# An encoder trunk: squares added on VectorE, rope and bias marks set later, modulation loaded with the latent heads

## The chip, the cores and the metric

The kernel runs on one core of one Trainium2 chip. The metric is device time in microseconds (us) of one execution. A core has several engines with queues of their own: TensorE (PE) multiplies matrices, VectorE (DVE) and ScalarE (ACT) work elementwise, SyncE (SP) issues the transfers, GpSimd (POOL) does almost nothing here. Each engine works its queue in order and waits on semaphores for the others.

## The reference

Two layers of a bidirectional encoder, for 256 tokens of width D = 2048 in float32. Each layer modulates with six vectors of 2048 values that come from one conditioning vector:

```python
cond = silu(c)
for l in range(2):
    mod = cond @ w_ada[l] + b_ada[l]            # w_ada[l]: 2048 x 12288
    sh_a, sc_a, g_a, sh_m, sc_m, g_m = split(mod, 6)
    h = rmsnorm(x) * (1 + sc_a) + sh_a
    proj = h @ w_in[l]                          # dq, dk, dv, cq, ckv, kr
    out_a = diff_attention(dq, dk, dv, positions, bias_table, lam, ...)  # 4 heads, relative bias
    q  = rmsnorm(cq, q_norm_g)  @ w_uq[l]       # latent attention: 8 heads, rope on 64 of 192
    kv = rmsnorm(ckv, kv_norm_g) @ w_ukv[l]
    out_b = mla_attention(q, rope(q), kv, rope(kr), ...)
    x = x + g_a * (concat(out_a, out_b) @ w_o[l])
    h = rmsnorm(x) * (1 + sc_m) + sh_m
    x = x + g_m * (square(relu(h @ w_mlp_in[l])) @ w_mlp_out[l])
return rmsnorm(x, final_norm_g)
```

## The kernel before

Activations lie transposed, features on the 128 partitions and the 256 tokens along the row, so that a weight tile is the fixed side of a matmul. Accuracy comes from splitting: `weights()` loads a raw float32 tile of 1 MB (2048 columns; w_f2 and w_n have 1536), ScalarE writes `hi` (L145), VectorE the remainder `lo` (L146), and `mac` (L181 to L183) does three matmuls for each 128x128 tile. Raw tiles have five buffers.

The modulation is no matmul. Each of the 192 tiles of w_ada, 1 MB, is loaded by `ada_load` (L289) into the same five buffers as the raw weights, multiplied with cond and summed along the row by one VectorE instruction in `ada_sums` (L297), followed by a short one that reads the accumulator and one that adds b_ada (L312, L314) into `mod`. `weights()` sums what has been loaded before, then adds `self.rate` to a credit and issues one such load for each whole unit of it. The rates differ by stage: RATE_H behind the head, RATE_A0 in layer 0's attention, RATE_A1 and RATE_A2 in layer 1's, RATE_K and RATE_M later. All loads go through SP's queue in the order of issue.

The order of the program in layer 0:

- `setup`, `bias_setup` (tables for the relative bias), the squares of x (ScalarE, L370, eight instructions of 128x512), `rstd` (32 matmul records with a matrix of 1/D, L580; square root; reciprocal, L583), `rope_setup` (cosine and sine, L533 to L552).
- The head: eight tiles k. Each loads two w_ada tiles of 1 MB, 0.384 MB of w_f1 and 0.512 MB of w_v1, sums the two, forms `ht` (VectorE, L381) and `hf` (ScalarE, L409), and runs 12 matmuls `pk` (L412) and 8 `pv` (L416). Behind tiles 2 and 4 stand the marks of the relative bias (`bias_marks`, 0 and 1: VectorE writes `oh`), behind 4 and 7 their products (`bias_products`, matmuls `pb`, L521 and L522, copied out as `bias` by ScalarE, L524).
- Sixteen w_b tiles of 1 MB, 48 `mac` records each.
- Layer 0: copies, `latent` for ckv, bias parts 2 and 3 (`bias_part` is marks and products together), `lambdas`, `rest_feats` (four w_f2 loads), `latent` for cq, then `probs(0)`, `keys` (w_kr and rope on the keys), `probs(1)`, two w_dv tiles, `probs(2)`, `up_k`, `probs(3)` and so on.
- The latent heads: `heads[hm]` has three steps for each of eight heads (scores, turn, values); the list `mla` puts them in ten groups so that heads overlap. The softmax there reads scores `psm` into `sm` (VectorE, L1093).
- w_oa (four tiles), w_ob (twelve tiles in pairs, residual x updated at L955 and its squares added), the norm (L580, L583, `ht` at L654) with sixteen w_n tiles, the MLP.

In setup, head and the w_b tiles, TensorE's order is the written one; on the other engines and elsewhere a scheduler orders instructions as they become ready by its own costs, inside what dependencies and buffers allow.

Of the kernel before, what the change touches and what calls it, by code (L numbers as in the profile page):

```python
# [20 lines left out]
D = 2048  # L21
# [78 lines left out]

RATE_H, RATE_A0, RATE_A1, RATE_A2, RATE_K, RATE_M = 1.25, 1.4, 0.5, 0.7, 0.6, 0.66


class Trunk:
# [31 lines left out]
    def weights(self, src, width=2048):  # L136
# [11 lines left out]
        self.ada_sums(ins)  # L148
        self.credit += self.rate
        while self.credit >= 1.0 and self.ada_todo:  # L150
            self.credit -= 1.0
            self.ada_load()
        return out

# [204 lines left out]
    def head(self):  # L359
# [5 lines left out]
        self.setup()  # L365
        self.bias_setup()
        sq = []
        for k in range(0, NK, 2):
            t = self.t("sqx")
            nc.scalar.activation(t, self.x[:, k : k + 2], AF.Square)  # L370
            sq += [t[:, 0], t[:, 1]]
        r = self.rstd(sq, D, True)
        self.rope_setup()
        sh, sc = self.mod[0, 0], self.mod[0, 1]
# [22 lines left out]
        for k in range(NSPLIT):  # L397
# [16 lines left out]
            for t in range(2):  # L414
                for cg in range(2):
                    mm(flat(vals[cg][t]), fs[k][:, t * P : (t + 1) * P], w[1][:, cg * 512 : cg * 512 + 512],  # L416
                       start=k == 0, stop=k == NSPLIT - 1)
            if k in MARKS:
                marks[MARKS[k]] = self.bias_marks(MARKS[k])
# [16 lines left out]

    def rest_feats(self, h):

        banks = self.open_banks(3)
        for p in range((NK - NSPLIT) // 2):  # L440
            for i, w in enumerate(self.weights(self.io["w_f2"][0, p], 1536)):
                k = NSPLIT + 2 * p + i
                for j in range(6):
                    self.mac(banks[j // 2][:, j % 2], w, j * P, P, h[k], k == NSPLIT and j % 2 == 0, k == NK - 1 and j % 2 == 1, True)
        qs = 1.0 / math.sqrt(128.0)
        for ps, t, s in zip(banks, self.part_f, (-1.0, qs, -1.0)):
            self.nc.vector.scalar_tensor_tensor(t, ps, s, t, ALU.mult, ALU.add)
        return self.part_f
# [123 lines left out]

    def rstd(self, acc, n, plain=False):

        nc = self.nc
        ps = self.bank("pn")[:, 0]
        if not plain:
            acc = acc[:2] + acc[3:]
        for i, a in enumerate(acc):
            nc.tensor.matmul(ps, self.mean[n], a, start=i == 0, stop=i == len(acc) - 1)  # L580
        r = self.cp.tile([P, T], F32, tag="rstd", name=self.name("rstd"), bufs=2)
        nc.scalar.activation(r, ps, AF.Sqrt, bias=self.eps)
        nc.vector.reciprocal(r, r)  # L583
        return r
# [115 lines left out]
    def layer(self, l, acc, st):  # L700
# [70 lines left out]
        for i in range(HM + 2):  # L771
            for s in range(3):
                if 0 <= i - s < HM:
                    mla.append(heads[i - s][s])
        gkv = self.vec[:, V_KVG + 2 * l : V_KVG + 2 * l + 2]
        gq = self.vec[:, V_QG + 4 * l : V_QG + 4 * l + 4]
        if l == 0:
# [3 lines left out]
            ckv += self.latent([ckr], gkv)  # L781
            self.bias_part(2)
            self.bias_part(3)
            self.lambdas()
            k2, q3, k3 = self.rest_feats(h)
            cq += self.latent(cqr, gq)
            kk += [k2, k3]
            q.append(q3)
            probs(0)()
            keys()  # L790
            probs(1)()
# [3 lines left out]
        else:  # L795
# [14 lines left out]
            self.rate = RATE_A2  # L810
        up_k()
        probs(3)()
# [19 lines left out]
        self.ada_need(l, 2, NK - 1)  # L832
        banks = self.open_banks(2)
        self.by_k(banks, [io["w_oa"][l, 0]], self.mo, 0, NK)
        for f in (av[0][1], av[1][1], av[2][0], av[3][0]):
# [386 lines left out]
```

## Time and profile before

| | us |
|---|---|
| median of 3 runs | 2275.76 (2272.86 to 2278.68) |
| the profiled execution | 2278.85 |
| its span | 2277.1 |
| TensorE busy | 2185.3 |
| VectorE busy | 1624.1 |
| ScalarE busy | 1157.1 |
| mean granted TensorE clock | 0.979 |

The profile is of one execution. Times in it count from the start of the span; durations are in us, or in ns where said. A group row gives line, engine, operation, output <- input and shape, then busy time and mean; an arrow in brackets gives the idle time before an instruction and what ended it. Accumulating instructions of VectorE show as two records, the second being the read of the accumulator. Matmuls in float32 show as more records than the program has instructions.

### The profile page before, as it was taken

Reading aid. Unit: us, or ns where it says so; the run is one execution under the profiler, and the core shown is the slowest. Engines: PE = TensorE matmul, PEld = TensorE weight load, DVE = VectorE, ACT = ScalarE, POOL = GpSimd, SP = SyncE. Lnnn points to the kernel's source line nnn. Section 1 sums busy time; section 2 is a strip of 40 time slices with the busy share of each in tenths; the row PEclk is TensorE's granted clock in tenths of the full one; section 3 lists DMA queues with packets and bytes.
Section 4 is the critical chain, followed back from the end, with each engine's and each line's share of the span. In section 5 each row is a group of like instructions: output and inputs, shape, how many; then the busy total and the mean of one; then the engine's idle time right before and its main releaser. Section 6 shows DMA issues by size and latency. Waiting matters only on the chain.

```text
span 2277.1 us, 31049 instructions
## 1 busy us (share of the span) xinstructions
PE 2185.3 (96%) x12346; PEld 1910.4 (84%) x12346; DVE 1624.1 (71%) x2161; ACT 1157.1 (51%) x1707; POOL 22.9 (1%) x43
## 2 busy tenths in 40 slices
PE   7996899879999999999999999999999999999997
PEld 4795778879888888888888898999888888888886
DVE  7786986897778778778899886677644544555555
ACT  3435565245446446445446656546645535544643
POOL 0000000000000000000001000000000000000000
PEclk9997999999999999999999999999999999999998
DMA  9795685879888888887876775665555555555551
GB/s 392 288 371 211 259 314 206 327 279 336 331 316 320 310 313 323 328 322 298 324 298 245 285 263 213 222 239 187 192 196 185 193 195 185 185 203 189 196 189 56
DMA packets 83812, 585.40 MB, mean 257 GB/s; under 512 B 9297, under 2 KB 9681, under 8 KB 17361
## 3 DMA queue, kind: packets, MB, share of 16 engines
q1 hardware_dynamic: 83666, 583.42, 69.0%
q8 instruction: 96, 1.57, 0.3%
q14 instruction: 50, 0.41, 0.1%
HBM read 581.28 MB, written 2.10 MB: 256 GB/s over the span
## 4 chain that ended last, share of the span: by engine, by line
PE 85%; DVE 9%; DMA 3%; ACT 2%; issue 1%; DVEq 0%; ACTq 0%
PE ps L202 20%; PE ps L205 11%; PE py L923 10%; PE py L925 10%; PE py L927 10%; DVE ada L297 3%; DVE lo L146 2%; PE pk L181 2%; PE pk L183 2%; PE pk L182 2%; PE ps L183 1%; PE ps L182 1%; PE ps L181 1%; DMA raw<-in_w_b 1%; PE pv L416 1%
## 5 line engine op out<-in xcount | busy, mean ns | idle before, releaser
L146 DVE TENSOR_TENSOR lo<-raw,hi 128x1024 fp32r<-128x1024 f32 (+1 forms) x724 | 854.8, 1195 | 507.2 <-ACT hi L145 346.4
L145 ACT ACTIVATE hi<-raw 128x1024 fp32r<-128x1024 f32 (+1 forms) x724 | 744.8, 1037 | 699.3 <-PE py L927 371.3
L202 PE MATMUL ps<-h,hi 128*128 128x512 f32 x2016 | 472.1, 391 | 0.0
L202 PEld LDWEIGHTS ps<-h,hi 128*128 128x128 f32 x2016 | 375.2, 188 | 75.7
L297 DVE SCALAR_TENSOR_TENSOR ada<-ada,cond 128x2048 f32<-128x2048 f32 x192 | 437.8, 2284 | 0.0
L923 PE MATMUL py<-hi,hid 128*128 128x512 f32 x1024 | 326.1, 389 | 0.0
L927 PE MATMUL py<-hi,hid 128*128 128x512 f32 x1024 | 325.7, 389 | 0.0
L925 PE MATMUL py<-lo,hid 128*128 128x512 f32 x1024 | 325.7, 389 | 0.0
L205 PEld LDWEIGHTS ps<-h,lo 128*128 128x128 f32 x2016 | 250.2, 192 | 4.9
L205 PE MATMUL ps<-h,lo 128*128 128x256 f32 x2016 | 251.7, 283 | 0.0
L927 PEld LDWEIGHTS py<-hi,hid 128*128 128x128 f32 x1024 | 192.2, 188 | 40.0
L925 PEld LDWEIGHTS py<-lo,hid 128*128 128x128 f32 x1024 | 192.2, 188 | 39.8
L923 PEld LDWEIGHTS py<-hi,hid 128*128 128x128 f32 x1024 | 191.7, 188 | 39.2
L181 PE MATMUL pk<-h,hi 128*128 128x256 f32 x496 | 141.7, 286 | 5.8 <-ACT h L655 5.8
L183 PE MATMUL pk<-h,lo 128*128 128x256 f32 x496 | 142.0, 286 | 1.7 <-DVE lo L146 1.5
L182 PE MATMUL pk<-h,hi 128*128 128x256 f32 x496 | 141.7, 286 | 0.0
L181 PEld LDWEIGHTS pk<-h,hi 128*128 128x128 f32 x496 | 96.3, 195 | 6.6 <-ACT h L655 6.2
L183 PEld LDWEIGHTS pk<-h,lo 128*128 128x128 f32 x496 | 96.6, 195 | 2.8 <-DVE lo L146 2.5
L961 ACT ACTIVATE sum<-ps 128x256 f32<-128x256 f32 x110 | 42.1, 383 | 111.6 <-PE ps L205 111.5
L182 PEld LDWEIGHTS pk<-h,hi 128*128 128x128 f32 x496 | 96.5, 195 | 0.2
L175 DVE TENSOR_TENSOR hid<-relu,hid 128x256 fp32r<-128x256 f32 x128 | 48.2, 421 | 47.1 <-ACT hid L174 47.1
L181 PE MATMUL ps<-moh,hi 128*128 128x256 f32 x192 | 55.9, 291 | 6.7 <-ACT hi L145 6.7
(240 smaller groups left out, 2614.6 us busy)
## 6 DMA issues: line engine op xcount, KB each, us to landing
raw<-in_w_m SPq DMA_DIRECT2D x238, 1024.0 KB, 4.8
ada<-in_w_ada SPq DMA_DIRECT2D x192, 1024.0 KB, 5.2
raw<-in_w_ob SPq DMA_DIRECT2D x24, 1024.0 KB, 5.7
raw<-in_w_b SPq DMA_DIRECT2D x16, 1024.0 KB, 6.8
raw<-in_w_q SPq DMA_DIRECT2D x16, 1024.0 KB, 5.1
raw<-in_w_dv SPq DMA_DIRECT2D x12, 1024.0 KB, 5.9
raw<-in_w_n SPq DMA_DIRECT2D x16, 768.0 KB, 5.9
raw<-in_w_oa SPq DMA_DIRECT2D x8, 1024.0 KB, 5.4
```

Of the source, the lines that this page charges most:

```text
L145: nc.scalar.activation(hi, v, AF.Copy)
L146: ins = nc.vector.tensor_tensor(lo, v, hi.bitcast(F32), ALU.subtract)
L175: self.nc.vector.tensor_tensor(lo, val[:, i], hi.bitcast(F32), ALU.subtract)
L181: mm(ps, hi, x[0], start=first, stop=False, skip_group_check=shared)
L182: mm(ps, hi, x[1], start=False, stop=False, skip_group_check=shared)
L183: mm(ps, lo, x[0], start=False, stop=last, skip_group_check=shared)
L202: mm(ps.rearrange("p a b -> p (a b)"), part(w, 0, k), both, start=k == 0, stop=False)
L205: mm(ps[:, 0], part(w, 1, k), x, start=False, stop=k == nk - 1)
L297: ins = nc.vector.scalar_tensor_tensor(w, w, 1.0, self.cond, ALU.mult, ALU.mult, accum_out=acc[:, i : i + 1])
L923: mm(o, xh[:, tok], hi[:, part[j]], start=start, stop=False)
L925: mm(o, xh[:, tok], lo[:, part[j]], start=False, stop=False)
L927: mm(o, xl[:, tok], hi[:, part[j]], start=False, stop=stop)
```

## The change

Squares of x: `sumsq`, which the later norms use, squares on ScalarE and adds on VectorE, so `rstd` gets two rows (L585 of the changed kernel, four records) in place of sixteen tiles, and its argument `plain` goes. `bias_setup` moves behind head tile 1, `rope_setup` out of the head into layer 0. The bias parts 2 and 3 are taken apart: marks first, products behind a half of `rest_feats`. `keys` stands ahead of `probs(0)`, and `up_k` of layer 0 ahead of `probs(1)`. In layer 0 each of the ten groups of latent-head steps ends with `tick()`, which sums the modulation tiles loaded before and adds RATE_S to the credit; RATE_A0 falls to 1.2, and from w_oa on layer 0 loads at RATE_O = 0.6.

```diff
@@ -98,7 +98,7 @@
 NNORM = 12
 
 
-RATE_H, RATE_A0, RATE_A1, RATE_A2, RATE_K, RATE_M = 1.25, 1.4, 0.5, 0.7, 0.6, 0.66
+RATE_H, RATE_A0, RATE_S, RATE_O, RATE_A1, RATE_A2, RATE_K, RATE_M = 1.25, 1.2, 1.3, 0.6, 0.5, 0.7, 0.6, 0.66
 
 
 class Trunk:
@@ -146,11 +146,18 @@
             ins = nc.vector.tensor_tensor(lo, v, hi.bitcast(F32), ALU.subtract)
             out.append((hi, lo))
         self.ada_sums(ins)
-        self.credit += self.rate
+        self.more(self.rate)
+        return out
+
+    def more(self, rate):
+        self.credit += rate
         while self.credit >= 1.0 and self.ada_todo:
             self.credit -= 1.0
             self.ada_load()
-        return out
+
+    def tick(self):
+        self.ada_sums()
+        self.more(RATE_S)
 
     def raw(self, src, width):
         raw = self.wp.tile([P, width], F32, tag="raw", name=self.name("raw"), bufs=5)
@@ -363,14 +370,10 @@
         flat = lambda ps: ps.rearrange("p a b -> p (a b)")
         qs = 1.0 / math.sqrt(128.0)
         self.setup()
-        self.bias_setup()
-        sq = []
+        acc = None
         for k in range(0, NK, 2):
-            t = self.t("sqx")
-            nc.scalar.activation(t, self.x[:, k : k + 2], AF.Square)
-            sq += [t[:, 0], t[:, 1]]
-        r = self.rstd(sq, D, True)
-        self.rope_setup()
+            acc = self.sumsq(acc, self.x[:, k : k + 2])
+        r = self.rstd(acc, D)
         sh, sc = self.mod[0, 0], self.mod[0, 1]
         feats = self.open_banks(3)
         vals = [[self.bank("pv") for _ in range(2)] for _ in range(2)]
@@ -415,6 +418,8 @@
                 for cg in range(2):
                     mm(flat(vals[cg][t]), fs[k][:, t * P : (t + 1) * P], w[1][:, cg * 512 : cg * 512 + 512],
                        start=k == 0, stop=k == NSPLIT - 1)
+            if k == 1:
+                self.bias_setup()
             if k in MARKS:
                 marks[MARKS[k]] = self.bias_marks(MARKS[k])
             if k in PRODUCTS:
@@ -434,14 +439,15 @@
                 ready(k + 2)
         return h, banks
 
-    def rest_feats(self, h):
-
-        banks = self.open_banks(3)
-        for p in range((NK - NSPLIT) // 2):
+    def rest_feats(self, h, ps, banks):
+
+        for p in ps:
             for i, w in enumerate(self.weights(self.io["w_f2"][0, p], 1536)):
                 k = NSPLIT + 2 * p + i
                 for j in range(6):
                     self.mac(banks[j // 2][:, j % 2], w, j * P, P, h[k], k == NSPLIT and j % 2 == 0, k == NK - 1 and j % 2 == 1, True)
+
+    def rest_sums(self, banks):
         qs = 1.0 / math.sqrt(128.0)
         for ps, t, s in zip(banks, self.part_f, (-1.0, qs, -1.0)):
             self.nc.vector.scalar_tensor_tensor(t, ps, s, t, ALU.mult, ALU.add)
@@ -570,12 +576,11 @@
         nc.vector.tensor_tensor(acc[2], acc[2], t, ALU.add)
         return acc
 
-    def rstd(self, acc, n, plain=False):
+    def rstd(self, acc, n):
 
         nc = self.nc
         ps = self.bank("pn")[:, 0]
-        if not plain:
-            acc = acc[:2] + acc[3:]
+        acc = acc[:2] + acc[3:]
         for i, a in enumerate(acc):
             nc.tensor.matmul(ps, self.mean[n], a, start=i == 0, stop=i == len(acc) - 1)
         r = self.cp.tile([P, T], F32, tag="rstd", name=self.name("rstd"), bufs=2)
@@ -772,6 +777,8 @@
             for s in range(3):
                 if 0 <= i - s < HM:
                     mla.append(heads[i - s][s])
+            if l == 0:
+                mla[-1] = lambda f=mla[-1]: (f(), self.tick())
         gkv = self.vec[:, V_KVG + 2 * l : V_KVG + 2 * l + 2]
         gq = self.vec[:, V_QG + 4 * l : V_QG + 4 * l + 4]
         if l == 0:
@@ -779,15 +786,22 @@
             kk += [self.copy(ps, "k", -1.0) for ps in banks[5:7]]
             q.append(self.copy(banks[7], "q", qs))
             ckv += self.latent([ckr], gkv)
-            self.bias_part(2)
-            self.bias_part(3)
-            self.lambdas()
-            k2, q3, k3 = self.rest_feats(h)
+            marks = self.bias_marks(2)
+            banks = self.open_banks(3)
+            self.rest_feats(h, (0, 1), banks)
+            self.bias_products(2, marks)
             cq += self.latent(cqr, gq)
+            marks = self.bias_marks(3)
+            self.rope_setup()
+            self.rest_feats(h, (2, 3), banks)
+            k2, q3, k3 = self.rest_sums(banks)
             kk += [k2, k3]
             q.append(q3)
+            self.bias_products(3, marks)
+            self.lambdas()
+            keys()
             probs(0)()
-            keys()
+            up_k()
             probs(1)()
             for kq in (2, 3):
                 val(0, kq)()
@@ -808,7 +822,7 @@
                     cq += self.latent(cqr, gq)
             keys()
             self.rate = RATE_A2
-        up_k()
+            up_k()
         probs(3)()
         up_q(0)
         turn(0)()
@@ -831,6 +845,8 @@
         g = self.mod[l, 2]
         self.ada_need(l, 2, NK - 1)
         banks = self.open_banks(2)
+        if l == 0:
+            self.rate = RATE_O
         self.by_k(banks, [io["w_oa"][l, 0]], self.mo, 0, NK)
         for f in (av[0][1], av[1][1], av[2][0], av[3][0]):
             f()
```

The instructions as the scheduler then orders them, with buffer numbers behind the names. VectorE at the start of the head, before (`ang`, `kk`, `rr`, `cc` are rope's, `rstd` the reciprocal, `ada` the modulation sums, `ht` the first tile's input):

```order
L297 SCALAR_TENSOR_TENSOR ada_232,macc_84<-ada_232,cond 128x2048
L540 SCALAR_TENSOR_TENSOR rr_201<-kk_200,rr_201 128x256
L583 RECIPROCAL rstd_196<-rstd_196 128x256
L540 SCALAR_TENSOR_TENSOR rr_201<-kk_200,rr_201 128x256
L312 SCALAR_TENSOR_TENSOR mod_83<-macc_84,vec 128x1
L540 SCALAR_TENSOR_TENSOR rr_201<-kk_200,rr_201 128x256 x4
L297 SCALAR_TENSOR_TENSOR ada_256,macc_82<-ada_256,cond 128x2048
L543 TENSOR_SCALAR rr_201<-rr_201 128x256
L314 TENSOR_TENSOR mod_81<-macc_82,vec 128x1
L547 TENSOR_SCALAR cc_216<-rr_201 128x256
L381 SCALAR_TENSOR_TENSOR ht_243<-x,mod_83,rstd_196 128x256
```

and now (`acc` are the additions of squares):

```order
L576 TENSOR_TENSOR acc_142<-acc_142,sqx_159 128x512
L576 TENSOR_TENSOR acc_142<-acc_142,sqx_162 128x512
L304 SCALAR_TENSOR_TENSOR ada_178,macc_82<-ada_178,cond 128x2048
L321 TENSOR_TENSOR mod_81<-macc_82,vec 128x1
L304 SCALAR_TENSOR_TENSOR ada_180,macc_84<-ada_180,cond 128x2048
L588 RECIPROCAL rstd_168<-rstd_168 128x256
L319 SCALAR_TENSOR_TENSOR mod_83<-macc_84,vec 128x1
L384 SCALAR_TENSOR_TENSOR ht_191<-x,mod_83,rstd_168 128x256
L481 TENSOR_SCALAR ih_229<-pos 128x264
```

Rope's rows and one modulation sum no longer stand around the reciprocal; two sums stand directly ahead of it, and the first tile's `ht` directly behind it.

ScalarE about head tiles 4 and 5, before (`sq` are from the bias marks, `bias` the copies of the products, `h` the splits for w_b):

```order
L508 ACTIVATE sq_430<-rel_398,K 128x512
L508 ACTIVATE sq_434<-rel_398,K 128x512
L524 ACTIVATE bias<-pb_438 32x512 x4
L409 ACTIVATE hf_384<-ht_471,mod_81 128x256
L409 ACTIVATE hf_496<-ht_497,mod_81 128x256
L388 ACTIVATE h_556<-hf_242 128x256
```

and now:

```order
L514 ACTIVATE sq_399<-rel_367,K 128x512
L514 ACTIVATE sq_403<-rel_367,K 128x512
L412 ACTIVATE hf_353<-ht_440,mod_81 128x256
L530 ACTIVATE bias<-pb_407 32x512 x4
L412 ACTIVATE hf_465<-ht_466,mod_81 128x256
L391 ACTIVATE h_525<-hf_190 128x256
```

The `hf` of the next tile stood behind the four copies of the bias products and now stands ahead of them.

VectorE in the latent heads, before (`sm` is the softmax's, `r` its reciprocal, `lo` a split of w_dv):

```order
L1093 TENSOR_SCALAR sm_2561,mxm_2562<-psm_2560 128x256
L146 TENSOR_TENSOR lo_2660<-raw_2657,hi_2659 128x1024
L146 TENSOR_TENSOR lo_2664<-raw_2657,hi_2663 128x1024
L1093 TENSOR_SCALAR sm_2561,mxm_2562<-psm_2560 128x256
L297 SCALAR_TENSOR_TENSOR ada_2587,macc_88<-ada_2587,cond 128x2048
L1015 RECIPROCAL r_2570<-tot_2569 128x2
L1093 TENSOR_SCALAR sm_2635,mxm_2636<-psm_2634 128x256
L314 TENSOR_TENSOR mod_87<-macc_88,vec 128x2
L297 SCALAR_TENSOR_TENSOR ada_2589,macc_90<-ada_2589,cond 128x2048
L1093 TENSOR_SCALAR sm_2635,mxm_2636<-psm_2634 128x256
L146 TENSOR_TENSOR lo_2764<-raw_2761,hi_2763 128x1024
```

and now:

```order
L1109 TENSOR_SCALAR sm_2547,mxm_2548<-psm_2546 128x256
L304 SCALAR_TENSOR_TENSOR ada_2773,macc_90<-ada_2773,cond 128x2048
L1109 TENSOR_SCALAR sm_2547,mxm_2548<-psm_2546 128x256
L304 SCALAR_TENSOR_TENSOR ada_2829,macc_90<-ada_2829,cond 128x2048
L1031 RECIPROCAL r_2556<-tot_2555 128x2
L146 TENSOR_TENSOR lo_2763<-raw_2760,hi_2762 128x1024
L1109 TENSOR_SCALAR sm_2626,mxm_2627<-psm_2625 128x256
L319 SCALAR_TENSOR_TENSOR mod_89<-macc_90,vec 128x2
L304 SCALAR_TENSOR_TENSOR ada_2859,macc_88<-ada_2859,cond 128x2048
L1109 TENSOR_SCALAR sm_2626,mxm_2627<-psm_2625 128x256
L146 TENSOR_TENSOR lo_2767<-raw_2760,hi_2766 128x1024
L1031 RECIPROCAL r_2635<-tot_2634 128x2
```

More modulation sums stand between the softmax's rows. In all there are 14 between the first `sm` and the last head's output, where 7 were.

VectorE in w_ob, before (`x` is the residual, `acc` its squares, `lo` the splits of w_ob):

```order
L146 TENSOR_TENSOR lo_3434<-raw_3427,hi_3433 128x1024
L297 SCALAR_TENSOR_TENSOR ada_3377,macc_88<-ada_3377,cond 128x2048
L146 TENSOR_TENSOR lo_3498<-raw_3495,hi_3497 128x1024
L314 TENSOR_TENSOR mod_87<-macc_88,vec 128x2
L146 TENSOR_TENSOR lo_3502<-raw_3495,hi_3501 128x1024
L297 SCALAR_TENSOR_TENSOR ada_3439,macc_90<-ada_3439,cond 128x2048
L955 SCALAR_TENSOR_TENSOR x<-ps_3363,mod_85,x 128x256 x2
L570 TENSOR_TENSOR acc_3356<-acc_3356,sqx_3491 128x512
L146 TENSOR_TENSOR lo_3561<-raw_3558,hi_3560 128x1024
L146 TENSOR_TENSOR lo_3565<-raw_3558,hi_3564 128x1024
L297 SCALAR_TENSOR_TENSOR ada_3506,macc_90<-ada_3506,cond 128x2048
L297 SCALAR_TENSOR_TENSOR ada_3508,macc_88<-ada_3508,cond 128x2048
```

and now:

```order
L576 TENSOR_TENSOR acc_3375<-acc_3375,sqx_3379 128x512
L146 TENSOR_TENSOR lo_3512<-raw_3509,hi_3511 128x1024
L146 TENSOR_TENSOR lo_3516<-raw_3509,hi_3515 128x1024
L304 SCALAR_TENSOR_TENSOR ada_3453,macc_88<-ada_3453,cond 128x2048
L146 TENSOR_TENSOR lo_3571<-raw_3568,hi_3570 128x1024
L971 SCALAR_TENSOR_TENSOR x<-ps_3382,mod_85,x 128x256 x2
L146 TENSOR_TENSOR lo_3575<-raw_3568,hi_3574 128x1024
L576 TENSOR_TENSOR acc_3375<-acc_3375,sqx_3505 128x512
L146 TENSOR_TENSOR lo_3637<-raw_3634,hi_3636 128x1024
L146 TENSOR_TENSOR lo_3641<-raw_3634,hi_3640 128x1024
L304 SCALAR_TENSOR_TENSOR ada_3578,macc_88<-ada_3578,cond 128x2048
```

Before, a sum followed each pair of splits, or two did; now one follows two pairs. Between the first w_ob residual and the last there are 7 sums, where 16 were.

On TensorE the two `pn` rows behind the w_b tiles were followed by the bias products and are now followed by w_f2's `mac` rows. In the norm behind w_ob, one modulation sum stood between the reciprocal and `ht`; now none does. On SP, 65 instead of 55 modulation loads stand ahead of the first w_oa tile, 3 instead of 6 between it and w_ob, 7 instead of 16 between w_ob and w_n, so 75 instead of 77 ahead of w_n.

## The prediction

> **What bounds the kernel now.** I read the page's busy table and chain first, then busy time by stage, then the waits and groups inside the stages that the change touches. Page, parts 1 and 4 (share of the span in brackets):
>
> ```profile
> PE 2185.3 (96%) x12346; PEld 1910.4 (84%) x12346; DVE 1624.1 (71%) x2161; ACT 1157.1 (51%) x1707; POOL 22.9 (1%) x43
> PE 85%; DVE 9%; DMA 3%; ACT 2%; issue 1%; DVEq 0%; ACTq 0%
> ```
>
> TensorE is idle for 2277.1 − 2185.3 = 92 us in all; a change that takes no multiplications away can win from that and from slow clock only. Where it is idle, by stage (each engine's busy us with its instruction count, then TensorE's granted clock, DMA share, GB/s):
>
> ```profile
> core 0: us, PE busy (x) PEld busy (x) DVE busy (x) ACT busy (x) POOL busy (x), PEclk, DMA share, GB/s
> 0.00:30.10 30.10, 16.34 (x41) 9.91 (x41) 17.54 (x37) 14.12 (x21) 1.02 (x9) 0.92 0.93 363
> 30.10:93.20 63.10, 60.22 (x192) 39.59 (x193) 49.45 (x84) 25.21 (x47) 0.00 (x0) 0.93 0.84 342
> 93.20:188.50 95.30, 93.61 (x769) 92.38 (x767) 83.42 (x99) 39.27 (x49) 0.00 (x0) 1.00 0.94 355
> 188.50:251.70 63.20, 42.52 (x250) 37.27 (x251) 46.66 (x71) 33.97 (x49) 0.53 (x1) 0.78 0.54 201
> 251.70:303.70 52.00, 44.58 (x242) 36.94 (x241) 50.68 (x108) 28.18 (x58) 0.00 (x0) 0.93 0.71 267
> 303.70:357.20 53.50, 48.00 (x242) 39.83 (x242) 37.60 (x74) 34.17 (x76) 0.00 (x0) 0.94 0.68 256
> 357.20:388.00 30.80, 30.80 (x236) 29.60 (x235) 21.31 (x29) 19.19 (x44) 0.00 (x0) 1.00 0.52 191
> 388.00:476.80 88.80, 75.85 (x582) 73.31 (x581) 75.21 (x89) 27.51 (x32) 0.00 (x0) 0.96 0.88 328
> 476.80:484.30 7.50, 1.40 (x4) 0.59 (x4) 6.68 (x9) 2.73 (x6) 0.00 (x0) 0.67 0.95 378
> ```
>
> The stages are: setup; the eight head tiles; the sixteen w_b tiles; bias, w_f2 and latents of layer 0; its keys and probabilities; its latent heads; w_oa; w_ob; the norm. Idle TensorE adds to 13.8 + 2.9 + 1.7 + 20.7 + 7.4 + 5.5 + 0 + 13.0 + 6.1 = 71 of the 92 us, and the change acts on these stages alone, the w_b tiles and the rest of the program keeping their order.
>
> **1. Setup and head (−5.5 us, between −2 and −9).** Rows of the timeline and one group:
>
> ```profile
> 10.35 3.74 ACT L370 ACTIVATE sqx<-x 128x512 f32<-128x512 f32 x7
> 11.02 9.18 PE L580 MATMUL pn<-sqx,mean 128*128 128x256 f32 x32 [1.20 <-ACT sqx L370]
> 22.43 1.74 DVE L583 RECIPROCAL rstd<-rstd 128x256 f32<-128x256 f32 x1
> 29.02 0.48 DVE L381 SCALAR_TENSOR_TENSOR ht<-x,mod,rstd 128x256 f32<-128x256 f32 x1
> 30.10 5.49 PE L412 MATMUL pk<-hf,w 128*128 128x256 f32 x12 [9.90 <-ACT hf L409]
> 189.72 1.10 PE L580 MATMUL pn<-acc,mean 128*128 128x256 f32 x4 [1.25 <-issue]
> L570 DVE TENSOR_TENSOR acc<-acc,sqx 128x512 f32<-128x512 f32 x2 | 1.4, 686 | 0.0
> L297 DVE SCALAR_TENSOR_TENSOR ada<-ada,cond 128x2048 f32<-128x2048 f32 x63 | 143.5, 2284 | 0.0
> L297 DVE DVE_READ_ACCUMULATOR ada<-ada,cond 128x1 f32 x62 | 5.2, 83 | 0.0
> L540 DVE SCALAR_TENSOR_TENSOR rr<-kk,rr 128x256 f32<-128x256 f32 x6 | 2.5, 413 | 0.1
> ```
>
> The 32 matmul records that sum the squares end at 11.02 + 9.18 = 20.2. Their place is taken by seven additions of 0.69 us, 4.8 us in all, that start behind the second square, near 10.9, and end at about 15.6 (the squares themselves end at 14.1); the four records of 1.10 us then end at 16.7, 3.5 us earlier. In the new order of VectorE two modulation sums (2.28 + 0.08 each) stand between the additions and the reciprocal, so it starts at 15.6 + 4.7 = 20.3 instead of 22.43 (the square root has its 2.2 us, as before from 20.2 to 22.43, beside them), and directly behind it, 1.74 us later, stands the first ht: at 22.0 instead of 29.02, because rope's rows and a third sum, which lay between the two, are gone. By the 1.1 us from ht to the first matmul, tile 0 begins at about 23.1 instead of 30.10: −7.
>
> Not all of it lasts. VectorE is full there, and what rope leaves (13 instructions, at the 0.41 of its row some 5 us, an estimate) bias_setup takes up again behind tile 1: eight instructions, four of them at the 0.69 us of the row of equal size, some 4 us. The next tiles' sums are then the pace, and the lead at tile 2 is 2 to 3 us. At tile 5 there is a second, separate gain:
>
> ```profile
> 20.00:40.00 20.00, 10.10 (x26) 6.79 (x26) 19.61 (x35) 5.41 (x8) 0.00 (x0) 0.74 1.02 424
> 65.53 0.48 DVE L381 SCALAR_TENSOR_TENSOR ht<-x,mod,rstd 128x256 f32<-128x256 f32 x1
> 66.87 2.39 ACT L524 ACTIVATE bias<-pb 32x512 f32<-32x512 f32 x4 [5.05 <-PE pb L522]
> 69.17 0.49 ACT L409 ACTIVATE hf<-ht,mod 128x256 f32<-128x256 f32 x1
> 69.71 4.53 PE L412 MATMUL pk<-hf,w 128*128 128x256 f32 x12 [2.88 <-ACT hf L409]
> 74.08 3.60 PE L416 MATMUL pv<-w,hf 128*128 128x512 f32 x8
> 77.51 2.75 PE L412 MATMUL pk<-hf,w 128*128 128x256 f32 x12
> ```
>
> Its ht is ready at 66.0, but hf waits on ScalarE behind four bias copies; in the new order hf stands ahead of them. That saves the 2.88 us wait and the 4.53 − 2.75 = 1.8 us of slow matmuls behind it, 4.7 together, of which the lead of 2 to 3 is partly the same time. I take −5.5. The shallow end (−2) is tile 5's wait with nothing of the start, the deep end (−9) is the whole 7 with the 1.8.
>
> On the slow matmuls, the Trainium skill's page "TensorE: Matmul & The Clock Gate", section "HAM oscillation — how this bites in real kernels", speaks against this change: if a short burst of matmuls waits longer than about 3.4 us for its data each time, each burst starts at half clock. The row above agrees, with a shorter wait: 4.53 instead of 2.75 us after 2.88. By that rule a head paced by VectorE in bursts of 6 us would run one tile more at 4.53: the sum below would be 2261 by the rule, and is 2259 without it.
>
> **2. Bias, w_f2 and latents, 188.5 to 251.7 (+1.8, between −6 and +4).** Waits of TensorE in the stage (total, times, longest):
>
> ```profile
> PE pb L521 <- DVE oh L510: 19.4, 3, 15.0
> ```
>
> The pn records are now followed by w_f2's matmuls instead of the bias products, so the 15 us gap while VectorE writes the marks oh fills with work. But this is exchange: VectorE, 46.66 of 63.2 us busy, gets rope (+5), one more sum (+2.4) and the k rows that came later before (some 7, an estimate from the order with these rows' times), about 61 us. With the 97% of the next stage (50.68 of 52.00) that needs 63 to 65. The gap moves into several smaller ones. Fully hidden, −6; with all latencies exposed, +4.
>
> **3. Keys and probabilities (+1, 0 to +4):** two more sums, 4.7 us, on an engine 97% busy, less the reordering's relief for keys, which now stand ahead of probs(0).
>
> **4. Latent heads (+4, 0 to +10).** The ten ticks bring 14 sums instead of 7: 7 × 2.37 = 16.6 us, less some 2.6 us of weight splits that fall outside: 37.6 + 14 = 51.6 us of VectorE work in a stage of 53.5, idle 15.9 before. If TensorE got the share it has next to a full VectorE, 44.58/52.00 = 0.857, its 48.0 us would need 56.0, that is +2.5. The idle time lay in short waits on ScalarE and TensorE which a 2.3 us sum overshoots, so I go to +4. Loads: the modulation's have 53.5 us at 0.68 share, room for 7 MB (17 us at 424 GB/s) but not much more. w_oa, already without a wait, gives −0.5.
>
> **5. w_ob (−15, between −10 and −18.5).** This carries the forecast. The same twelve tiles run in both layers. Busy time of layer 1's stage, in the columns of the table above; then the modulation sums alone in both layers' stages (VectorE's busy us and its count, two records to a sum); then TensorE's waits in layer 0:
>
> ```profile
> 1479.30:1549.60 70.30, 70.30 (x588) 70.30 (x587) 47.83 (x62) 31.96 (x38) 0.00 (x0) 1.00 0.62 222
> 388.00:476.80 88.80, 37.73 (x34) 0.96 0.88 328
> 1479.30:1549.60 70.30, 6.88 (x6) 1.00 0.62 222
> PE ps L181 <- ACT hi L145: 6.7, 4, 2.6
> PE ps L183 <- DVE lo L146: 3.7, 5, 0.8
> ```
>
> In layer 1, with 3 sums, TensorE never waits and the tiles take 70.3 us. In layer 0, with 16 to 17 sums, VectorE is 75.21 of 88.8 us busy, a sum gives back the buffer into which the next weights load, and the weights' splits stand behind the sums. With rate 0.6, 7 sums remain: VectorE has some 75.2 − 9.5 × 2.37 = 52.7 us of work, nearer to layer 1's 47.8 than to 75.2, and the DMAs 19 MB in 70 us, 270 GB/s, which the rows above exceed. 88.8 − 70.3 = 18.5 us at most, and I give back 3.5 for the four sums that are more than in layer 1. −10 is TensorE's two listed waits (6.7 + 3.7) alone, without clock and tail.
>
> **6. Norm (−2.2).** Between reciprocal and ht there stood one sum, which is now elsewhere:
>
> ```profile
> 479.45 1.75 DVE L583 RECIPROCAL rstd<-rstd 128x256 f32<-128x256 f32 x1
> 481.11 2.23 DVE L297 SCALAR_TENSOR_TENSOR ada<-ada,cond 128x2048 f32<-128x2048 f32 x1
> 483.26 0.88 DVE L654 SCALAR_TENSOR_TENSOR ht<-x,mod,rstd 128x256 f32<-128x256 f32 x2
> ```
>
> The modulation ends as it would: 75 loads instead of 77 stand ahead of w_n, so two sums more fall into later stages, where TensorE is the limit and VectorE free. I cost that at nothing; if the cover were gone it is 4.7 us.
>
> **Sum:** −5.5 + 1.8 + 1 + 4 − 0.5 − 15 − 2.2 = −16.4 us. The profiled execution took 2278.85 us, 3.1 above the median of the runs (2275.76), so 2262.4 by the profile and 2259 by the median.
>
> **The rivals.** (a) *Larger gain*: short stalls that I charge are hidden. Stage 2 really loses its wait (−5 instead of +1.8) and the 14 sums fit into the 15.9 us of idle VectorE (0 instead of +4): −27.2, 2249. For it: the idle time exists; against: it is spread in pieces under 3 us. (b) *The head is held by its transfers*: each head tile needs 3 MB, 7.1 us at the 424 GB/s of the row from 20 to 40 us, where the DMA share is 1.02, against some 6.3 us of matmuls (2.75 + 3.60). An earlier start then only reaches the wait for tile data sooner. With nothing gained there: −10.9, 2265. Against: tile 5 waited for ScalarE, not for data. (c) *Slower*: VectorE's queue is in order, and a tick's sum waits there for its load with the softmax behind it. A tick comes every 53.5/10 = 5.35 us; a 2.45 us part of a megabyte pair's landing exposed at each of the ten gives +24.5, on top of all 14 us of the added work exposed: +38.5 instead of +4, in all +18.1, 2294. It turns the kernel slower from +27 in that stage on. For it: the loads are issued only one tick earlier; against: the sums in the new order stand a group or more behind their loads, and the stage's DMAs are a third idle. (d) *The rate does nothing*: the w_ob stage stays slow for its weights' transfers. Then the sum keeps −1.4, 2274; layer 1's row speaks against it.
>
> **How the numbers follow.** A measurement of this kernel tells about 0.3%, 6.8 us, from no change, so faster means under 2269. Forecast 2259 (its own range 2253 to 2266): 0.52; (a) 0.2; (b) 0.14; (c) 0.06; (d) 0.08. (a) and the forecast are faster, (b) mostly; (d) is the same, (c) slower with a little same: 0.83, 0.12, 0.05. The range 2245 to 2271 holds the forecast, (a) but its deepest part, and (b).
>
> **What would show it.** Right: first head matmul near 23 and w_b near 88; no wait near 15 us behind the w_b tiles, but VectorE over 90% busy until the latent heads end; 52 to 60 us for the latent heads with 14 sums; w_ob's tiles in 70 to 73 us without a wait for hi; ht directly behind the reciprocal. Wrong: a DMA as VectorE's releaser in the latent heads, or w_ob over 78 us.

## The result, and the profile after

| | before | after |
|---|---|---|
| median, us | 2274.49 (2272.86 to 2278.68, 4 runs) | 2250.97 (2249.45 to 2251.70, 4 runs) |
| profiled execution: time, span, us | 2278.85, 2277.1 | 2249.45, 2247.6 |
| TensorE, VectorE busy, us | 2185.3, 1624.1 | 2167.3, 1627.8 |

The ratio is 0.9893, 95% interval 0.9876 to 0.9910: 23.5 us faster. The prediction said 2259 (2245 to 2271). VectorE does as much work as before. Of the 29.4 us that the span lost, 11.5 are idle time of TensorE (91.8 us before, 80.3 after) and 18.0 its busy time: 7.1 of these are the matmul records of the squares (setup, 16.34 to 9.24 us busy), and the largest part of the rest is slow clock in w_ob (75.85 to 69.20 us busy, granted clock 0.96 and 1.00).

Busy time by stage of the kernel after, in the columns used for before (each engine's busy us and count, TensorE's granted clock, DMA share, GB/s). The stages: setup; head; w_b; bias, w_f2, latents and now keys; probabilities; latent heads; w_oa; w_ob; norm.

```profile
0.00:22.89 22.89, 9.24 (x13) 3.67 (x13) 12.49 (x22) 10.09 (x16) 1.02 (x9) 1.00 0.88 336
22.89:86.84 63.95, 60.18 (x193) 39.41 (x193) 54.14 (x91) 26.20 (x48) 0.00 (x0) 0.97 0.93 387
86.84:182.09 95.25, 93.07 (x770) 92.28 (x768) 83.32 (x99) 40.60 (x52) 0.00 (x0) 1.00 0.93 362
182.09:236.50 54.41, 37.25 (x234) 35.05 (x235) 51.76 (x84) 31.35 (x46) 0.81 (x1) 0.81 0.67 245
236.50:291.50 55.00, 44.01 (x238) 36.21 (x237) 51.56 (x109) 28.18 (x56) 0.00 (x0) 0.84 0.73 269
291.50:355.40 63.90, 54.03 (x269) 45.38 (x268) 59.21 (x100) 35.47 (x81) 0.00 (x0) 0.95 0.84 324
355.40:385.40 30.00, 30.00 (x231) 28.77 (x230) 16.75 (x26) 18.72 (x41) 0.00 (x0) 1.00 0.47 174
385.40:454.60 69.20, 69.20 (x579) 69.20 (x578) 53.17 (x62) 28.89 (x32) 0.00 (x0) 1.00 0.78 281
454.60:460.30 5.70, 2.06 (x9) 1.15 (x7) 4.54 (x7) 2.44 (x6) 0.00 (x0) 1.00 0.79 293
```

Two things are to be seen. w_ob has no idle TensorE left, at full clock: 69.20 us for what took 86.2 from its first matmul to its last. And from 182 to 355 us VectorE is 51.76 + 51.56 + 59.21 = 162.5 of 173.3 us busy, 94%.

The same ledger with stages cut at the same first matmuls in both profiles (`psm` is the latent heads' first score, so rows four and five do not depend on where keys stand); the last column is the prediction's term:

| from, to | before | after | difference | predicted |
|---|---|---|---|---|
| start, first head tile | 30.1 | 22.9 | −7.2 | −7 |
| head tiles, to w_b | 63.1 | 64.0 | +0.9 | +1.5 |
| w_b tiles | 96.5 | 95.3 | −1.3 | 0 |
| to first `psm` | 109.1 | 109.4 | +0.3 | +2.8 |
| latent heads | 59.5 | 63.9 | +4.4 | +4 |
| w_oa | 29.7 | 29.9 | +0.3 | −0.5 |
| w_ob and norm, to w_n | 96.3 | 75.0 | −21.3 | −17.2 |
| w_n | 71.5 | 70.7 | −0.8 | 0 |
| everything behind | 1721.2 | 1716.6 | −4.6 | 0 |

That is −29.4 in the spans, where the prediction's terms add to −16.4. The medians differ by 23.5: the profiled execution of before is 4.4 above its median, that of after 1.5 below, so differences of a few us in this table are partly scatter.

### The profile page after: what moved, and what is told of

Read it like the earlier page. It is cut to its first block, busy times and chain, and to the rows that moved or that the text cites. A ratio compares the mean times of both kernels' runs of the same rounds, so it can differ in the third digit from the quotient of the medians.

```text
span 2247.6 us, 31016 instructions
## 1 busy us (share of the span) xinstructions
PE 2167.3 (96%) x12318; PEld 1899.0 (84%) x12318; DVE 1627.8 (72%) x2168; ACT 1153.5 (51%) x1704; POOL 20.4 (1%) x43
## 3 DMA queue, kind: packets, MB, share of 16 engines
q1 hardware_dynamic: 83666, 583.42, 69.7%
## 4 chain that ended last, share of the span: by engine, by line
PE 89%; DVE 7%; ACT 1%; DMA 1%; issue 1%; DVEq 0%; ACTq 0%; SPq 0%
PE ps L209 20%; PE ps L212 11%; PE py L941 10%; PE py L943 10%; PE py L939 10%; PE pk L190 2%; DVE ada L304 2%; PE pk L188 2%; PE pk L189 2%; PE ps L189 2%; PE ps L188 2%; PE ps L190 2%; DVE lo L146 1%; PE pv L259 1%; PE pv L260 1%; PE pv L261 1%
## 5 line engine op out<-in xcount | busy, mean ns | idle before, releaser
L190 PE MATMUL pa<-ah,lo 128*128 128x258 f32 x192 | 55.3, 288 | 4.6 <-DVE lo L146 4.6
```

Of the source, the lines that this page charges most:

```text
L190: mm(ps, lo, x[0], start=False, stop=last, skip_group_check=shared)
```

## The experiments

Twelve kernels, in three batches, with the kernel before measured in each (2273.7, 2275.4 and 2274.5 us). The first, second and third below are edits of the kernel before, the others of the changed kernel; "..." marks left out lines. A stage time below is from the profile of the run, between the first matmuls named.

**The modulation part alone**, on the kernel before: the rates and ticks, nothing of head or order.

```diff
-RATE_H, RATE_A0, RATE_A1, RATE_A2, RATE_K, RATE_M = 1.25, 1.4, 0.5, 0.7, 0.6, 0.66
+RATE_H, RATE_A0, RATE_S, RATE_O, RATE_A1, RATE_A2, RATE_K, RATE_M = 1.25, 1.2, 1.3, 0.6, 0.5, 0.7, 0.6, 0.66
...
+            if l == 0:
+                mla[-1] = lambda f=mla[-1]: (f(), self.tick())
...
+        if l == 0:
+            self.rate = RATE_O
         self.by_k(banks, [io["w_oa"][l, 0]], self.mo, 0, NK)
```

> Theory A (VectorE's pace): from the end of the w_b tiles to the end of the latent heads VectorE sets the time, in w_oa and w_ob TensorE does, so a modulation sum is worth its 2.37 us where it is taken from w_ob and costs most of it in the latent heads. The modulation part alone then takes w_ob to 69 to 71 us (-17 with 2 us of its tail) and makes the latent heads 8 to 10 us longer: 2274.5 - 19 + 9 = about 2264 us. Rival B (the order of layer 0 and the head carry the gain, the rates only shift the load): w_ob gets faster but the latent heads and the norm give all of it back, 2270 to 2276 us.

2255.87 us, ratio 0.9920 (0.9901 to 0.9939): −17.8 of the 23.5 us. w_ob took 69.3 us, the tail with the norm 5.7 instead of 10.1, the latent heads 62.8 instead of 59.5. The rates do carry the gain; rival B falls. Theory A has the stages right and one size wrong: eight sums more make the latent heads 3.3 us longer, not 8 to 10, so the time is 8 us under its 2264.

**The squares alone**, rope and bias tables left in place.

```diff
...
-            sq += [t[:, 0], t[:, 1]]
-        r = self.rstd(sq, D, True)
+            acc = self.sumsq(acc, self.x[:, k : k + 2])
+        r = self.rstd(acc, D)
```

> The squares on VectorE alone, rope and bias tables where they were. Theory A: the 32 matmul records were not what the first tile waited for, VectorE's rows ahead of the first ht were (three sums, the reciprocal, rope); they still stand there, so the first head matmul comes at 28 to 29 us instead of 30.1 and the time is 2272 to 2275 us. Rival C (the matmuls of the squares held the start): first head matmul near 26.5, 2270 us.

2274.02 us, ratio 1.0001 (0.9988 to 1.0013): nothing. Its timeline of VectorE and TensorE at the start:

```profile
17.15 2.07 PE L578 MATMUL pn<-acc,mean 128*128 128x256 f32 x4 [7.30 <-DVE acc L568]
22.05 1.75 DVE L581 RECIPROCAL rstd<-rstd 128x256 f32<-128x256 f32 x1
31.18 0.48 DVE L379 SCALAR_TENSOR_TENSOR ht<-x,mod,rstd 128x256 f32<-128x256 f32 x1
33.50 5.04 PE L410 MATMUL pk<-hf,w 128*128 128x256 f32 x12 [14.27 <-ACT hf L407]
```

The matmul records of the squares end 1 us sooner, and the first tile starts 3.4 us later than before (I expected 1 to 2 sooner): between the reciprocal and ht rope's rows and two sums remain. Yet w_b begins at 91.3 instead of 93.2, since VectorE is then ahead for the tiles that follow. The squares' matmuls held nothing.

**The head part alone**: the squares as above, bias tables behind tile 1, rope behind bias part 3, rates and order of before.

```diff
-        self.bias_setup()
...
-        self.rope_setup()
...
+            if k == 1:
+                self.bias_setup()
...
             self.bias_part(3)
+            self.rope_setup()
```

> The head part alone (squares, bias tables behind tile 1, rope behind bias part 3 in layer 0), rates and order of layer 0 as before. Theory A: first head matmul near 23, w_b near 87 (-6); rope's 5 us come back in the stage behind the w_b tiles, where TensorE waits for VectorE: +3 to +5. 2270 to 2273 us. Rival: rope is hidden there, since VectorE is idle a quarter of that stage: 2268 us.

2269.76 us, ratio 0.9982 (0.9973 to 0.9992): −3.9. First tile at 22.9, w_b at 86.9, as forecast; between the w_b tiles and `psm` it takes 110.8 instead of 109.1, less than the 3 to 5 expected, and the time lies between the two expectations.

**The changed kernel with the old order of layer 0**: modulation and head part together, without the order.

```diff
-            marks = self.bias_marks(2)
+            self.bias_part(2)
+            self.bias_part(3)
+            self.rope_setup()
+            self.lambdas()
...
+            probs(0)()
             keys()
-            probs(0)()
-            up_k()
             probs(1)()
...
-            up_k()
+        up_k()
```

> The changed kernel with layer 0's order as before: both bias parts whole, rope behind them, w_f2 unsplit, probs(0) ahead of keys, up_k in its old place. Theory A: the order part fills TensorE's 15 us wait but VectorE's work is the same, so its worth is what of VectorE's idle time it fills: 16 us of idle in that stage, about a third of it, 5 to 8 us. 2256 to 2259 us. If the order is worth nothing: 2251. If it carries the gain (rival B): 2262 or more.

2255.95 us, ratio 0.9918 (0.9900 to 0.9937): the same as the modulation part without the head part. The head's lead at w_b, 3.5 us over that kernel, is gone at w_oa (360.4 and 359.6 us). It goes at one wait, at the first scores of the latent heads, where TensorE waits for the queries' rope `qr`, which VectorE works out; without the head part this wait is 2.1 us:

```profile
PE psm L1104 <- DVE qr L1015: 7.6, 1, 7.6
```

From the w_b tiles to w_oa VectorE is 159.1 of 176.2 us busy with the head part and 152.9 of 172.4 without: the work of rope, moved there, is not hidden. So the order part is worth the last 5 us, to 2250.97.

**keys and up_k back in their places**, marks, products and w_f2 split as changed.

```diff
-            keys()
             probs(0)()
-            up_k()
+            keys()
             probs(1)()
...
-            up_k()
+        up_k()
```

> The changed kernel with keys behind probs(0) and up_k behind probs(2), as before; marks, products and w_f2 stay split. The order part is worth 5 us (2256.0 with the whole old order). If the marks' split carries it: 2251 to 2252 us. If the move of keys and up_k does: 2255 to 2256.

2243.54 us, ratio 0.9864 (0.9849 to 0.9879): outside both expectations, 7 us *faster* than the changed kernel. Of the order part, the split of marks, products and w_f2, with rope between, gains about 12 us (from 2255.95) and the move of keys and up_k loses 7. TensorE's waits in the probabilities and latent heads of the changed kernel, the lines that differ most:

```profile
PE psm L1108 <- DVE qr L1019: 4.9, 1, 4.9
PE psc L1041 <- DVE mx L1042: 4.7, 3, 3.6
PE pv L259 <- DVE mx L1042: 2.0, 1, 2.0
```

and from the end of the w_b tiles to w_oa with keys and up_k back:

```profile
PE psm L1107 <- DVE qr L1018: 2.1, 1, 2.1
PE psc L1040 <- DVE mx L1041: 0.2, 1, 0.2
```

`psc` are the scores of the differential heads and `mx` their maximum on VectorE. One wait goes the other way: `pt` waits 3.3 us for ScalarE in the changed kernel and 4.9 here. With keys ahead, the first `psc` comes at 236.5 instead of 226.9 us, and up_k's matmuls are spent before the late heads' softmax, which then has less to cover it, as I read these waits; that is not shown. What is measured: the stretch from the w_b tiles to `psm` takes 109.4 with the move and 99.5 without. It also holds 17 modulation sums with the move and 15 without (VectorE 103.4 and 96.5 us busy), so a part of the difference may be sums that come earlier. keys and up_k were not moved one by one.

**Fewer sums in the latent heads, more in w_oa and w_ob.**

```diff
-RATE_S, RATE_O = 1.3, 0.6
+RATE_S, RATE_O = 0.6, 0.9
```

> The changed kernel with RATE_S 0.6 instead of 1.3 and RATE_O 0.9 instead of 0.6: 58 instead of 65 modulation loads ahead of w_oa, 15 instead of 10 between there and w_n. So far the latent heads with w_oa took 93.8 us with 8.5 sums more than before, which took 89.2: about half a microsecond for each sum, where a fully exposed one costs 2.37. Theory A (a sum there costs a part of its time, one in w_oa or w_ob nothing): latent heads 3 to 4 us shorter, w_ob as it is at 69 to 70 us, about 2247 us. If sums there are fully exposed: 16 us shorter, 2235. Rival (w_ob is at the edge of VectorE, 53 of 69 us busy, and its loads): w_ob 5 us or more longer, 2250 to 2256.

2248.40 us, ratio 0.9884 (0.9865 to 0.9903). The latent heads take 60.3 instead of 63.9, w_ob 69.28 as it was: half a microsecond for each of the seven sums that left the heads, as expected. In w_ob stand eleven sums now instead of seven.

**Without the cut to 0.6, and with 1.4 again.**

```diff
-            self.rate = RATE_O
+            self.rate = RATE_A0    # 1.2
```

> The changed kernel without the cut to 0.6: RATE_A0 = 1.2 stays through w_oa and w_ob (84 instead of 75 modulation loads ahead of w_n). Theory A: the sums in w_ob set its time through the buffers; w_ob goes from 69 us back to 83 to 87, the norm gets its late sum back: 2266 to 2270 us. Rival (w_ob got faster because the order and the ticks left it better supplied): w_ob stays below 75 us, 2252 to 2256.

```diff
-            self.rate = RATE_O
+            self.rate = 1.4
```

> The changed kernel with 1.4, the rate of before, from w_oa on. At 1.2 w_ob took 73.4 us, below the knee 69.3, in the kernel before (1.4) 86.2. If the rate alone sets it: 84 to 88 us here too, and 2268 to 2275 us in all. If VectorE's work alone counts: (1.4 - 1.13) x 2.37 x 12 = 7.7 us over 69.3, that is 77. If the kernel before was slow there for what it brought from the stages ahead (a debt of loads): 77 or less and 2260 to 2264 us.

2260.83 us, ratio 0.9939 (0.9916 to 0.9961), and 2268.13 us, ratio 0.9972 (0.9960 to 0.9985). VectorE's time on the sums in w_ob (busy us and records, two to a sum; then granted clock, DMA share, GB/s) at 0.6, 0.9, 1.2 and 1.4:

```profile
385.38:454.66 69.28, 16.05 (x14) 1.00 0.78 281
381.75:451.03 69.28, 25.22 (x22) 1.00 0.91 337
387.06:460.41 73.35, 29.65 (x26) 0.98 0.92 346
385.03:467.45 82.42, 35.19 (x32) 0.98 0.92 341
```

w_ob as a stage, from first to last matmul, at 0.9 (the run before these):

```profile
381.75:451.03 69.28, 69.28 (x579) 69.28 (x578) 61.98 (x73) 29.07 (x32) 0.00 (x0) 1.00 0.91 337
```

At 1.2:

```profile
387.06:460.41 73.35, 71.49 (x581) 71.23 (x580) 65.04 (x77) 27.05 (x30) 0.00 (x0) 0.98 0.92 346
```

At 1.4:

```profile
385.03:467.45 82.42, 74.04 (x582) 71.67 (x580) 69.97 (x83) 26.26 (x29) 0.00 (x0) 0.98 0.92 341
```

The longest wait of ScalarE in that stage (total, times, longest), at 0.9:

```profile
ACT hi L145 <- PE ps L189: 33.0, 20, 2.0
```

and at 1.4:

```profile
ACT hi L145 <- DMA raw<-in_w_ob: 24.2, 8, 4.4
```

At 0.9 ScalarE's split waits for TensorE to give back its hi and lo buffers, so TensorE is the limit. At 1.4 it waits 24.2 us for w_ob itself to land, and the loads in turn are issued late, SP waiting for VectorE to give a raw buffer back (L296 issues a modulation load, L164 a weight load):

```profile
SPq L296 <- DVE lo L146: 30.4, 10, 5.0
SPq L164 <- DVE ada L304: 19.9, 9, 4.1
```

At 0.9 SP waits in the same way, 24.9 us in its longest line, and TensorE is not held. At 1.4 VectorE is 85% busy, less than the 89% at 0.9, while the transfers have a share of 0.92, at 0.9 already 0.91. Both expectations miss the size of the stage: at 1.2 it takes 73.4 us, under theory A's 83 to 87 and as the rival had it, but the time lies above the rival's; at 1.4 its 82.4 lies between the 77 from VectorE's work and the 84 to 88 from the rate. The kernel with the squares alone, also at 1.4, has 82.9 us there and the kernel before 86.2, so the rate makes w_ob slow with and without the rest of the change, but VectorE's work is not the whole of it. What limits lies in the loop of load, split and sum through the five raw buffers; whether the buffers or the transfers give way first was not tried.

**Without the ticks.**

```diff
-                mla[-1] = lambda f=mla[-1]: (f(), self.tick())
+                pass
```

> The changed kernel without the ten ticks, rates as changed: 62 instead of 75 modulation loads ahead of w_n. Theory A: latent heads 4 to 5 us shorter, w_ob stays at 69; but the norm needs 80 sums by its last tile and has some 72 by then, so eight loads come at once and TensorE waits 20 to 25 us for them at w_n: 2265 to 2275 us. If the loads are hidden beside w_n: 2246.

2262.98 us, ratio 0.9949 (0.9932 to 0.9966). Waits of TensorE from 440 to 560 us:

```profile
PE pk L188 <- ACT h L660: 13.7, 5, 3.4
```

and w_n as a stage:

```profile
452.58:542.73 90.15, 78.37 (x577) 76.63 (x578) 82.39 (x107) 34.82 (x54) 0.00 (x0) 0.91 0.88 343
```

The latent heads gain 6.9 us, w_n loses 19.4: its matmuls wait for `h`, into which ScalarE adds the modulation. The waits are shorter than the 20 to 25 us expected, and slow clock comes on top (TensorE 78.4 us busy in w_n instead of 70.7), so the time is 2 us under theory A's range. Loads have a due time; here the ticks move them and cannot simply be left out.

**Rope between the w_b tiles.**

```diff
-            self.rope_setup()
...
+            if k == 6:
+                self.rope_setup()
```

> The changed kernel with rope written between the w_b tiles (behind the seventh) instead of in layer 0. There VectorE is 83.3 of 95.2 us busy and TensorE never waits for it, behind them VectorE is 95% busy. Theory A: rope's 5 us are hidden in w_b, and the stretch behind gets 2 to 5 us shorter: 2247 us. Rival (VectorE's idle time in w_b lies in pieces that the splits need): w_b 3 to 5 us longer, 2251 or more.

2247.53 us, ratio 0.9881 (0.9866 to 0.9895), so 3.4 better. Both expectations come true in part: the w_b tiles take 99.8 instead of 95.3 (TensorE waits there for `lo` 3.8 us in all, 0.8 before), the stretch from them to w_oa 165.0 instead of 173.4.

**Both together**, and with yet fewer sums in the heads:

```diff
-RATE_S, RATE_O = 1.3, 0.6
+RATE_S, RATE_O = 0.6, 0.9     # second kernel: 0.3, 1.1
```

> Both improvements together: rope between the w_b tiles, RATE_S 0.6, RATE_O 0.9. Alone they gave 2247.5 and 2248.4 us where the changed kernel had 2251.0. If they act on different stages (rope on the stretch behind w_b, the sums on the latent heads) they add: 2245 us. If both only relieve VectorE in the same stretch, the second finds TensorE's own time there already: 2247 us.

> As the run before with RATE_S 0.3 and RATE_O 1.1 (55 loads ahead of w_oa, 18 between there and w_n). A w_ob tile takes TensorE 69.3/12 = 5.77 us, VectorE's own work for it is (53.17 - 16.05)/12 = 3.1 us, so there is room for 2.7 us or 1.13 sums of 2.37 us a tile. By that knee 1.1 still fits: w_ob 69 to 70 us, latent heads 1 to 2 us shorter than with 0.6, 2243 to 2245 us. If the limit is softer (buffers, waits on transfers): w_ob 71 us or more, and the time is 2246 to 2250.

2242.66 us, ratio 0.9860 (0.9843 to 0.9876), and 2250.12 us, ratio 0.9894 (0.9879 to 0.9909). The first adds up a little better than expected, 8.3 us under the changed kernel. The second misses: w_ob goes to 70.7 us and the tail with the norm from 5.7 back to 9.2, so 1.1 is already past the rate up to which sums are free, which I had worked out as 1.13; and from the w_b tiles to w_oa it takes 1.9 us more, not less. The stretch from the w_b tiles to w_oa, in the first:

```profile
186.50:348.10 161.60, 131.04 (x737) 113.48 (x738) 140.83 (x257) 92.91 (x178) 0.53 (x1) 0.89 0.71 265
```

and in the second:

```profile
186.60:350.10 163.50, 132.75 (x739) 114.91 (x739) 134.89 (x250) 92.50 (x178) 0.53 (x1) 0.90 0.65 244
```

VectorE falls from 140.8 to 134.9 us and the time does not: at 87% and 83% it is the waits between engines that are left, not VectorE's sum of work. Rope in w_b, the later sums and keys with up_k in their old places were not run together; each of the two fastest kernels has only one side of it.

## Why the prediction was right, and where its sizes were off

**The head (−5.5) was right by most of its steps**, −6.4 at w_b. The rows at the start, as forecast for 23.1 and 22.0 us:

```profile
20.00 1.75 DVE L588 RECIPROCAL rstd<-rstd 128x256 f32<-128x256 f32 x1
21.81 0.48 DVE L384 SCALAR_TENSOR_TENSOR ht<-x,mod,rstd 128x256 f32<-128x256 f32 x1
22.89 5.47 PE L415 MATMUL pk<-hf,w 128*128 128x256 f32 x12 [5.28 <-ACT hf L412]
47.60 4.47 PE L415 MATMUL pk<-hf,w 128*128 128x256 f32 x12 [3.77 <-ACT hf L412]
65.09 2.75 PE L415 MATMUL pk<-hf,w 128*128 128x256 f32 x12
```

The last two rows are tiles 3 and 5: tile 5 lost its wait and its slow matmuls, and tile 3 got both, since its ht stands behind two sums and the marks' rows on VectorE. That is what the rule on waits and half clock in the Trainium skill's page "TensorE: Matmul & The Clock Gate" ("HAM oscillation — how this bites in real kernels") had against the change: one burst of 4.47 us behind a wait of 3.77, about the 2 us that the prediction gave for it. The row of before, 4.53 us at a granted clock of 0.61 behind a wait of 2.88, shows that the page's figure of about 3.4 us is no lower bound here.

The lead of 7 us lasts longer than I said (7.3 at tile 2, not 2 to 3), is down to 1.6 at tile 4, and the whole 4.7 of tile 5 then comes on top. The four `pn` records took 2.08 us and not 1.10, at no cost, as the two sums beside them ended later. But what the head part wins at w_b reaches the end only where VectorE has room for rope: 3.9 us with the old rates, none with the new ones in the old order.

**Bias to probabilities (+1.8 and +1) was right in kind**: the 15 us wait is now 6.0 and 11.2:

```profile
PE pb L527 <- DVE oh L516: 11.2, 1, 11.2
PE pk L190 <- DVE lo L146: 6.0, 1, 6.0
```

The step that failed is inside it: I counted keys ahead of probs(0) as a relief. It costs, with up_k, 7 us, and the split of marks, products and w_f2, which I took for mere exchange, earns 12. That the ledger shows +0.3 where I had +2.8 is therefore luck: two effects that I did not have stand against each other.

**Latent heads (+4): +4.4, but not by its steps.** The sums grew from about 7 to about 15 there and no DMA appears as VectorE's releaser in that stage, so rival (c) did not come; its 2.45 us of an exposed landing has no row behind it. The prediction's stage runs from the first `sm` to the last output (53.5 us). In this cut the kernel after takes 55.5 us with VectorE 50.9 us busy, so the 56.0 from TensorE's share beside a full VectorE and the 51.6 of VectorE's work were right, and the 1.5 us that I added were not needed. The rest of the 4.4 lies between the first `psm` and the first `sm`, 7.7 us instead of 4.8: the wait of 4.9 us for `qr` shown above, which the prediction did not have.

**The other rivals.** (b) fell with the first tiles, whose lead reached w_b; (d) fell with w_ob. (a) named a time, 2249, close to the measured one, but by stalls hidden ahead of w_ob, and those stages cost 5.0 us in all (0.3 + 4.4 + 0.3). The profiled execution is 13 us under the sum (2262.4 by the profile): 4.6 of these lie behind the stages of the change, 4.1 in w_ob and norm, 2.5 in bias to probabilities, the rest in pieces of about 1 us.

**w_ob and norm (−15 and −2.2): −21.3, the largest term, and mis-sized.** I took 3.5 us back from the 18.5 that layer 1's stage left, for four sums more. Seven sums in w_ob cost nothing, nor do eleven. In the prediction's own cut w_ob went from 88.8 to 69.2 us, by 19.6: the 15, the 3.5, and 1.1 more, since layer 1's 70.3 us hold nine matmul records of the MLP (`pa`, 1.1 us). The norm went from 7.5 to 5.7 us. Its rows stand as forecast, ht directly behind the reciprocal:

```profile
457.46 1.75 DVE L588 RECIPROCAL rstd<-rstd 128x256 f32<-128x256 f32 x1 [1.02 <-ACT rstd L587]
459.25 1.28 DVE L659 SCALAR_TENSOR_TENSOR ht<-x,mod,rstd 128x256 f32<-128x256 f32 x3
```

**What lies behind (0): −4.6.** Half is a sum that left the start of layer 1, where VectorE is nearly full. That stage before:

```profile
1205.30:1275.20 69.90, 64.29 (x418) 59.74 (x418) 64.88 (x98) 40.89 (x70) 10.60 (x15) 0.95 0.78 275
```

and after:

```profile
1180.90:1248.20 67.30, 63.16 (x417) 58.60 (x418) 62.48 (x96) 40.19 (x70) 8.76 (x15) 0.97 0.73 270
```

The five kernels that have the rates and ticks of the change show it (67.2 to 67.4 us), those with the old rates do not (69.7 to 69.8), and other rates move it between 66.2 and 69.6: it follows where the credit falls due. Of the other half, 1.8 us are clock at the very end (below). I had said that moved loads meet a free VectorE behind; at this one place they do not.

## What to carry to other kernels

Work that paces one stage is worth moving into a stage that hides a part of it, even when its engine is then almost full there: here the price is about half a microsecond for each sum of 2.4 us in the latent heads, and nothing in w_ob up to a rate of 0.9. From 1.2 to 1.4 each further sum costs more than its own time (9.1 us for 5.5 us of sums). Look for that rate in the same stage of another layer, and take the stage's floor from there without a discount, less what else runs in it. When work is moved ahead on TensorE, ask what it was covering where it stood: moving keys and up_k cost 7 us, and the waits that grew with it are those for a softmax and for `qr`.

## What the runs showed of the hardware

The last norm's matmuls ran at two speeds behind the same wait. Timeline of the kernel before:

```profile
2261.79 2.07 PE L580 MATMUL pn<-acc,mean 128*128 128x256 f32 x4 [1.92 <-DVE acc L570]
2263.66 1.91 PE L580 MATMUL pn<-sqa,mean 128*128 128x256 f32 x4
```

After:

```profile
2234.50 1.13 PE L585 MATMUL pn<-acc,mean 128*128 128x256 f32 x4 [1.92 <-DVE acc L576]
2235.47 1.03 PE L585 MATMUL pn<-sqa,mean 128*128 128x256 f32 x4
```

With the sums later (RATE_S 0.6):

```profile
2231.04 2.08 PE L585 MATMUL pn<-acc,mean 128*128 128x256 f32 x4 [1.92 <-DVE acc L576]
2232.91 1.91 PE L585 MATMUL pn<-sqa,mean 128*128 128x256 f32 x4
```

The third kernel has the changed tail and the slow clock, so the 1.8 us do not belong to the changed instructions. In all fourteen profiles the wait is 1.92 us, and the eight records behind it take from 1.99 us (six kernels) to 3.78 (three). Ahead of the wait stand only eight transposes (`yt`), so the last other matmul ends 3.7 us before these rows in each of the three. Each kernel was profiled once, so whether one kernel shows both speeds is not known. The Trainium skill's page "TensorE: Matmul & The Clock Gate", section "Part 1: The HAM clock gate (the "warmup" mystery)", says that the window which watches TensorE's activity runs freely and does not start with the kernel; these rows agree with that, and no run here tests it.
